# A norm's factor spread over the partitions: diagonal and matmul, or a store to DRAM and a broadcast load

## The chip, the cores and the metric

The kernel runs on one core of a Trainium2 chip. The metric is the device time of one execution in microseconds, the median of several. Five engines work side by side, each through its own list of instructions in order: TensorE (PE in the profile, its weight loads PEld), VectorE (DVE), ScalarE (ACT), GpSimd (POOL) and SyncE (SP), which here only issues DMAs. An instruction that has to wait holds up everything behind it on its engine. ACT issues a few DMAs as well.

## What is computed

A trunk of two layers over 1024 tokens of width 1024. Each layer normalizes x, projects it, runs token attention (windowed in the first layer, a two-dimensional neighbourhood in the second) beside a cross-attention into 256 memory tokens, projects back, normalizes again and applies a SwiGLU of width 2816. A last norm ends it.

```python
def rmsnorm(x, g):
    x32 = x.astype(jnp.float32)
    y = x32 * lax.rsqrt(jnp.mean(x32 * x32, axis=-1, keepdims=True) + EPS)
    return (y * g.astype(jnp.float32)).astype(x.dtype)

mem_n = rmsnorm(mem, norm_mem)
for i in range(DEPTH):
    h = rmsnorm(x, norm_mix[i])
    ...
    x = x + jnp.concatenate([y_tok, y_mem], axis=-1) @ w_out[i]
    h = rmsnorm(x, norm_ffn[i])
    gu = h @ w_gate_up[i]
    x = x + (jax.nn.silu(gu[..., :D_FF]) * gu[..., D_FF:]) @ w_down[i]
return rmsnorm(x, norm_final)
```

The change touches only how the factor of a norm, one number for each token, reaches the places where it is multiplied in.

## The kernel before

**Layout.** x is held transposed: features on the 128 partitions in eight tiles `x[k]`, tokens along the free dimension, in two halves `f` of 512 tokens (`HS`). A float32 product is made of three matmuls of a rounded part and a rest: `hi` (ACT rounds) and `lo` (DVE subtracts, in some places POOL) split every operand, weights too, and L140, L1079 and L1510 are the three matmuls per block of the projections, of the gate-and-up products and of the down products.

**A norm.** `Norm.add` squares a tile on ACT and sums squares on DVE. `Norm.sums` lets PE sum over the partitions (L213, out `st`, 128 tokens on the partitions, one column per block of 128 tokens), DVE adds epsilon (L233, `nv`), POOL takes the power -1/2 (L234, `nr`). The factor now lies with one token on each partition. To bring it to every partition with tokens along the free dimension, DVE writes a diagonal matrix (L237, `diag`), and `Norm.scale` multiplies it with a matrix of ones on PE (L249, `bc`, a PSUM bank). `raw`, `split`, `finish` and `right_sides` multiply x by gain and factor from that bank (L256, L270, L1523, L1269). A norm over 512 tokens is called with n=512, the memory norm has 256, and the last two quarters (`ends`) have 256 each: twelve norms, twelve `bc` products.

**Which norm is where.** At the start the first half's projections are made of x without its factor; `unit_scale`, a copy of `bc` in SBUF, is multiplied into their results later (L488, `first_sums`, and L650). The memory norm's factor is copied to `scale` (L486). The second half's first norm is used in `split` for `hT`. In each layer the norm of the first half of the tokens before the SwiGLU is summed while the second half's output projection runs (L1245), and at the end of each layer the first half's next norm is summed within the last of seven down products (`i == 6`), which goes through six groups `g` of weight tiles (two each, the last one; PE takes group 4 together with group 5).

**Order.** The program is written in the order of the code, and the scheduler of the framework then sets each engine's list by its own estimate of when operands are ready, so neighbours on an engine may come from places of the code that lie apart. Tiles come from pools with a set number of buffers; a load into a buffer waits until the last reader of its previous content is done. Weight tiles are loaded by SP into a `raw` buffer (five of them in this part of a layer, shared with the output tiles `o`), split by ACT and DVE into one of three `whl` buffers, and then used by PE.

Of the kernel before, what the change touches and what calls it, by code (L numbers as in the profile page):

```python
# [9 lines left out]
F32 = mybir.dt.float32  # L10
# [7 lines left out]
P = 128  # L18
# [3 lines left out]
HS = 512  # L22
# [19 lines left out]
def trunk_kernel(ctx: ExitStack, tc: tile.TileContext, a: dict, out: bass.AP):  # L42
# [17 lines left out]
    nc = tc.nc  # L60
# [17 lines left out]
    memk_d = dr.tile([2, 2, P, 2 * NM], F32, name="memk_d")  # L78
    memv_d = dr.tile([2, P, S], F32, name="memv_d")
    bias_d = dr.tile([NH, P, 3 * P], F32, name="bias_d")  # L80

    ident = cst.tile([P, P], F32, name="ident")
    gains = cst.tile([P, 6, NK], F32, name="gains")
# [13 lines left out]
    def temp(name="t2k", n=HS):  # L97
        t = phase[0].tile([P, HS], F32, tag="t2k", name=name, bufs=phase[1])
        return t[:, :n] if n != HS else t
# [85 lines left out]
    class Norm:  # L185


        def __init__(self, n=HS, summed=NK, bank=ps_t):
            self.n, self.acc, self.xs, self.st, self.dg = n, [], {}, None, None
            self.summed, self.bank = summed, bank  # L190

        def add(self, xk, k=None):
# [27 lines left out]
            nc.vector.tensor_tensor(one, one, sq, op=ALU.add)  # L220
            self.acc.append(one)

        def sums(self):

            n, nb = self.n, self.n // P
            if len(self.acc) > 1:
                self.merge()
            for sq in self.acc:
                self.mean(sq)
            st = self.st  # L230
            v = sp.tile([P, 4], F32, tag="nv", name="nv", bufs=2)
            r = sp.tile([P, 4], F32, tag="nr", name="nr", bufs=2)
            nc.vector.tensor_scalar(v[:, :nb], st[:, :nb], EPS, None, op0=ALU.add)  # L233
            nc.gpsimd.tensor_tensor(r[:, :nb], v[:, :nb], neg_half[:, :nb], op=ALU.pow)  # L234
            self.r = r
            self.dg = temp("diag", n)
            nc.vector.tensor_tensor(  # L237
                self.dg.rearrange("p (b q) -> p b q", q=P),
                ident.unsqueeze(1).to_broadcast([P, nb, P]),
                r[:, :nb].unsqueeze(2).to_broadcast([P, nb, P]),  # L240
                op=ALU.mult,
            )

        def scale(self, bank=ps_o):

            if self.dg is None:
                self.sums()
            bc = bank.tile([P, HS], F32, tag="O" if bank is ps_o else "T", name="bc")[:, : self.n]
            nc.tensor.matmul(bc, ones, self.dg, start=True, stop=True)  # L249
            return bc  # L250
# [9 lines left out]

        def split(self, which, hs, lag=0):

            if self.dg is None:
                self.sums()
            for _ in range(lag):
                yield
            bc = self.scale()
            for k in range(NK):
                h = temp("h")
                nc.vector.scalar_tensor_tensor(  # L270
                    h, self.xs[k], gains[:, which, k : k + 1], bc, op0=ALU.mult, op1=ALU.mult
                )
                t = hp.tile([P, 2, HS], F32R, tag="h", name="hT")
                hi(t[:, 0], h)
                lo(t[:, 1], h, t[:, 0])
                hs[k] = t
                yield
# [9 lines left out]
    with tc.tile_pool(name="mp", bufs=1, reuse_waits="tile") as mp:  # L287
# [105 lines left out]
        run(steps(sums[1], wf[1], hT[0]))  # L393
        last = steps(sums[2], wf[2], hT[0])
        run_some(last, 4)
        norms[0].sums()
        mh = []
        mhl = mp.tile([P, NK, 2, NM], F32R, name="mhl")

# [64 lines left out]
        for i in range(8):  # L464
# [9 lines left out]
                split_wm(i + 2)  # L474
            mem_dense(i)
            if i == 0:
                nc.scalar.copy(unit_scale, norms[0].scale())
                norms[1].xs = {k: x[k][1] for k in range(NK)}
                parts = total(norms[1], [xp[k, 1] for k in range(0, NK, 2)])
                run_some(parts, 3)  # L480
            if i == 1:
                run(parts)
                run(total(mem_norm, [memt.rearrange("p k t -> p (k t)")[:, c : c + HS] for c in range(0, 2 * D, HS)], HS))
                mem_norm.sums()
            if i == 2:
                nc.scalar.copy(scale, mem_norm.scale())  # L486
                for n in range(3):
                    nc.vector.tensor_tensor(first_sums[n], sums[n], unit_scale, op=ALU.mult)  # L488
            if i == 3:
                norms[1].sums()  # L490
                nc.vector.tensor_scalar(nsink, sink, -1.0, None, op0=ALU.mult)
                todo = (None for j in range(4) for _ in finish_wm(j))
            if i == 4:
# [26 lines left out]
    for layer in range(2):  # L520
# [467 lines left out]
        with (  # L988
# [241 lines left out]
            for f in range(2):  # L1230
                for m in range(NK):
# [13 lines left out]
                    if f == 0 and m < NK - 1:  # L1245
                        load_y(1, pairs[m])
                    if f == 1 and m == 0:
                        norms[0].sums()
                        parts = norms[0].raw(2 + layer)
                    if f == 1:  # L1250
                        for _ in range(int(m > 0) + int(m == 6)):
                            k = next(parts)
                            B[k // 4][k % 4] = pair(x[k][0], h_op(k))
                        if 1 <= m <= 2:
# [259 lines left out]

            def finish(norm):

                norm.sums()
                yield
                bc = norm.scale()
                for k in range(NK):  # L1520
                    if k % 2 == 0:
# [58 lines left out]
            for at_, (i, g) in enumerate(dorder):  # L1580
# [15 lines left out]
                for c in quarter if last and not is_a else (slice(0, HS),):  # L1596
                    for m in range(4):
# [6 lines left out]
                        if c is quarter[1]:  # L1604
                            if m == 1:
                                end = finish_end(quarter[0])
                            if m > 0:
                                run_some(end, 1)
                if i == 6 and g > 0:
                    if g == 1:  # L1610
                        parts = norms[0].split(1, hT[0], 1) if is_a else finish(norms[0])
                    run_some(parts, 3 if g > 1 else 1)
                    if g < 5:
                        if is_a:
                            norms[1].add(x[g - 1][1], g - 1)
                        for c in () if is_a else quarter:
# [97 lines left out]
```

## Time and profile before

| | |
|---|---|
| median of 3 runs | 2120.81 us (2120.08 to 2121.54) |
| the profiled execution's own time | 2121.35 us |
| its span in the profile | 2119.5 us |
| PE busy | 2094.4 us (99%) |
| DVE busy | 1522.0 us (72%) |
| ACT busy | 1067.0 us (50%) |
| POOL busy | 575.1 us (27%) |
| moved by DMA | 287.28 MB, mean 136 GB/s |

The span runs from the first instruction to the end of the last one. A row of the timeline gives a start, a length, an engine, a line, the operation and its tiles and how many equal instructions were merged; in brackets the idle time of the engine before them and what ended it. SPq and ACTq are the sequencers of SP and ACT, that is, the issue of a DMA. Starts of matmuls are recorded, their ends are modelled. A float32 product such as `bc` is recorded as two matmuls.

### The profile page before, as it was taken

To read this page: it belongs to the slowest core of one execution; us is meant where nothing else is said; L and a number is where in the kernel's file an instruction comes from. 1 tells how busy PE (TensorE), PEld (TensorE's weight loads), DVE (VectorE), ACT (ScalarE), POOL (GpSimd) and SP (SyncE) were. 2 spreads that over 40 slices of the span, in tenths; PEclk is the share of its full clock that TensorE was granted. 3 is DMA by queue.
4 is the path that set the end of the run, shared out by engine and by line. 5 is a ranking of instruction groups with operands and counts; after the bars stand their busy time and mean duration, and the time that the engine had idled before them with its cause. 6 is when DMAs were issued, how large, how long until landed. Compare 5 with 4: busy or idle time off the path is not lost.

```text
span 2119.5 us, 29023 instructions
## 1 busy us (share of the span) xinstructions
PE 2094.4 (99%) x10316; PEld 1750.1 (83%) x10316; DVE 1522.0 (72%) x2477; ACT 1067.0 (50%) x2035; POOL 575.1 (27%) x614
## 2 busy tenths in 40 slices
PE   9999999999999999999999999999999999999997
PEld 7788888878888888888888888888788888888886
DVE  7787887787666666866776666667986666667675
ACT  6687775444434334344466665654543434344442
POOL 0344330234444430000233223203243444400000
PEclk9999999999999999999999999999999999999998
DMA  6421128332333227865232222275232333277562
GB/s 232 145 82 50 31 95 274 99 111 103 109 114 105 91 105 254 312 217 206 79 109 68 69 71 78 64 268 149 75 110 105 109 115 109 86 253 265 200 220 85
DMA packets 120913, 287.28 MB, mean 136 GB/s; under 512 B 12224, under 2 KB 20672, under 8 KB 120768
## 3 DMA queue, kind: packets, MB, share of 16 engines
q1 hardware_dynamic: 112880, 271.63, 38.1%
q10 hardware_dynamic: 7888, 13.79, 1.7%
q8 instruction: 82, 1.34, 0.3%
q14 instruction: 63, 0.52, 0.1%
HBM read 210.40 MB, written 68.94 MB: 132 GB/s over the span
## 4 chain that ended last, share of the span: by engine, by line
PE 91%; DVE 3%; ACT 2%; DMA 1%; issue 1%; POOL 1%; DVEq 0%; ACTq 0%; SPq 0%; POOLq 0%
PE X L1079 17%; PE Y L1079 16%; PE mm L140 15%; PE X L1510 11%; PE Y L1510 8%; PE po L140 8%; PE O L787 3%; PE S L724 3%; PE pT L767 3%; PE X L1161 2%; PE Y L1161 2%; PE mm L426 1%; DMA wd_kept<-in_w_dn 1%; PE bc L249 0%; POOL wS L1036 0%
## 5 line engine op out<-in xcount | busy, mean ns | idle before, releaser
L1079 PE MATMUL Y<-hB,wgu 128*128 128x512 f32 x1056 | 255.6, 391 | 0.8 <-ACT c L1099 0.8
L1079 PE MATMUL X<-hB,wgu 128*128 128x512 f32 x1056 | 254.8, 391 | 0.0
L1510 PE MATMUL X<-hB,wd 128*128 128x512 f32 (+1 forms) x1092 | 243.8, 384 | 0.9 <-DVE x L1474 0.9
L109 DVE TENSOR_TENSOR wgu<-wS,wgu 128x1024 fp32r<-128x1024 f32 (+1 forms) x124 | 153.0, 1234 | 121.7 <-ACT wgu L106 121.3
L1510 PEld LDWEIGHTS X<-hB,wd 128*128 128x128 f32 x1092 | 200.2, 188 | 41.7 <-issue 2.2
L1079 PEld LDWEIGHTS Y<-hB,wgu 128*128 128x128 f32 x1056 | 196.8, 188 | 43.4 <-ACT c L1099 1.6
L1079 PEld LDWEIGHTS X<-hB,wgu 128*128 128x128 f32 x1056 | 196.0, 188 | 39.8
L752 POOL TENSOR_SCALAR p<-p,stat 128x384 f32<-128x384 f32 (+1 forms) x256 | 139.5, 564 | 315.0 <-DVE stat L749 208.7
L140 PE MATMUL mm<-hT,wqk 128*128 128x512 f32 x672 | 199.2, 405 | 0.0
L106 ACT CAST wgu<-wS 128x1024 fp32r<-128x1024 f32 (+1 forms) x124 | 114.2, 923 | 149.7 <-POOL wS L1036 124.5
L140 PE MATMUL po<-yT,wo 128*128 128x512 f32 x768 | 185.7, 394 | 0.0
L1510 PE MATMUL Y<-hB,wd 128*128 128x512 f32 x792 | 180.7, 389 | 0.0
L1510 PEld LDWEIGHTS Y<-hB,wd 128*128 128x128 f32 x792 | 148.6, 188 | 31.5 <-DVE x L1474 0.4
L234 POOL TENSOR_TENSOR nr<-nv,neg_half 128x4 f32<-128x4 f32 (+1 forms) x12 | 13.4, 1116 | 586.5 <-DVE nv L233 582.6
L140 PEld LDWEIGHTS po<-yT,wo 128*128 128x128 f32 x768 | 142.4, 188 | 30.0 <-issue 1.0
L1079 PE MATMUL X<-hT,wgu 128*128 128x512 f32 x624 | 150.2, 391 | 0.0
L106 ACT CAST hB<-b_raw 128x512 fp32r<-128x512 f32 x154 | 89.3, 618 | 112.7 <-DMA b_raw<-b_d 95.9
L1036 POOL TENSOR_TENSOR wS<-wgu_raw 128x512 f32<-128x512 f32 x44 | 61.0, 1387 | 295.1 <-DVE wgu L109 295.1
L1079 PEld LDWEIGHTS X<-hT,wgu 128*128 128x128 f32 x624 | 116.9, 188 | 26.1
L739 ACT ACTIVATE p<-p,stat 128x256 f32<-128x256 f32 (+1 forms) x192 | 112.5, 587 | 49.2 <-DVE stat L735 47.0
L109 DVE TENSOR_TENSOR pl<-pT,ph 128x384 fp32r<-128x384 f32 (+1 forms) x256 | 118.8, 493 | 18.5 <-ACT ph L106 15.4
L1079 PE MATMUL Y<-hT,wgu 128*128 128x512 f32 x528 | 129.9, 391 | 0.0
(208 smaller groups left out, 4204.3 us busy)
## 6 DMA issues: line engine op xcount, KB each, us to landing
wgu_raw<-in_w_gu SPq DMA_DIRECT2D x92, 512.0 KB
wd_raw<-in_w_dn SPq DMA_DIRECT2D x70, 512.0 KB
b_raw<-b_d SPq DMA_DIRECT2D x70, 512.0 KB
b_d<-c SPq DMA_DIRECT2D x88, 256.0 KB
b_d<-t SPq DMA_DIRECT2D x66, 256.0 KB
wo_raw<-in_w_out SPq DMA_DIRECT2D x32, 512.0 KB
xr_d<-x ACTq DMA_DIRECT2D x32, 256.0 KB
xr<-xr_d SPq DMA_DIRECT2D x16, 512.0 KB
```

Of the source, the lines that this page charges most:

```text
L106: nc.scalar.copy(dst, src)
L109: (eng or nc.vector).tensor_tensor(dst, src, h.bitcast(F32), op=ALU.subtract)
L140: nc.tensor.matmul(ps[:, :n], l, r, start=start and i == 0 and j == 0, stop=stop and i == len(order) - 1 and j == 2,)
L724: nc.tensor.matmul(s_[:, :n], Q[self.h][:, qb * P : (qb + 1) * P], k, start=j == 0, stop=j == 1)
L739: nc.scalar.activation(p[:, :n], p[:, :n], AF.Exp, bias=m1, scale=-1.0, accum_out=s1)
L752: nc.gpsimd.tensor_scalar(p[:, :n], p[:, :n], ri[:, i : i + 1], 1.0, op0=ALU.mult, op1=ALU.mult)
L767: nc.tensor.transpose(tr[:, j * P : (j + 1) * P], p[:, j * P : (j + 1) * P], ident)
L787: nc.tensor.matmul(o[:, c0 : c0 + w * P], self.value(j), t[:, s0 : s0 + w].rearrange("p j q -> p (j q)"), start=j == js[0] and t is self.p ...
L1036: sub = lambda o, p_, q_: nc.gpsimd.tensor_tensor(o, p_, q_, op=ALU.subtract)
L1079: nc.tensor.matmul(ps, l, r, start=n in (0, 1, 3, 6) and k == 0 and i == 0, stop=k == 3 and i == 2, skip_group_check=True,)
L1161: nc.tensor.matmul(bank[:, at : at + h2], l, r, start=start and k == 0 and i == 0, stop=stop and k == 1 and i == 2, skip_group_check=True,)
L1510: nc.tensor.matmul(bank[:, c], l, r, start=i in (0, 1, 3, 6) and p == 0 and n == 0, stop=p == HF - 1 and n == 2, skip_group_check=True,)
```

## The change

`Norm.sums` takes a tile `into`. With it, no diagonal is written: SP stores the factors `r` (128 partitions by four, or by two) to a row `r_d` in DRAM, one token after the other, and loads that row into `into`, the same row for each of the 128 partitions. `scale` then returns this SBUF tile and issues no matmul. Seven of the twelve norms are called so: the first half's at the start (into `unit_scale`), the memory norm (into `scale`), the second half's at the start, the first half's before the SwiGLU of each layer, and the first half's at the end of each layer. The copies of `bc` to `unit_scale` and `scale` on ACT go. The five others keep the diagonal and the matmul.

Three places of the code move. At the start the second half's `sums` comes at `i == 2` in place of 3. Before the SwiGLU, the scaled tiles are made from `m == 2` on in place of 1, with two at m = 4 and 6. At the end of a layer `sums` comes after group 0 of `i == 6` in place of group 1, and the first use one step later than before.

```diff
+    r_d = [dr.tile([1, HS], F32, name=f"r_d{i}") for i in range(7)]
+    used = []
...
-        def sums(self):
+        def sums(self, into=None):
...
             self.r = r
+            if into is not None:
+                row = r_d[len(used)]
+                used.append(row)
+                nc.sync.dma_start(row[:, :n].rearrange("o (b p) -> p (o b)", p=P), r[:, :nb])
+                nc.sync.dma_start(into[:, :n], row[:, :n].to_broadcast([P, n]))
+                self.bc = into[:, :n]
+                return
             self.dg = temp("diag", n)
...
         def scale(self, bank=ps_o):
+            if self.bc is not None:
+                return self.bc
...
-        norms[0].sums()
+        norms[0].sums(unit_scale)
...
             if i == 0:
-                nc.scalar.copy(unit_scale, norms[0].scale())
...
-                mem_norm.sums()
+                mem_norm.sums(scale)
             if i == 2:
-                nc.scalar.copy(scale, mem_norm.scale())
+                norms[1].sums(temp("bc"))
...
             if i == 3:
-                norms[1].sums()
...
                     if f == 1 and m == 0:
-                        norms[0].sums()
+                        norms[0].sums(temp("bc"))
...
-                        for _ in range(int(m > 0) + int(m == 6)):
+                        for _ in range(int(m > 1) + int(m in (4, 6))):
...
             def finish(norm):
-                norm.sums()
-                yield
+                norm.sums(temp("bc"))
+                for _ in range(2):
+                    yield
...
-                if i == 6 and g > 0:
-                    if g == 1:
-                        parts = norms[0].split(1, hT[0], 1) if is_a else finish(norms[0])
+                if i == 6:
+                    if g == 0:
+                        if is_a:
+                            norms[0].sums(temp("bc"))
+                            parts = norms[0].split(1, hT[0], 2)
+                        else:
+                            parts = finish(norms[0])
                     run_some(parts, 3 if g > 1 else 1)
-                    if g < 5:
+                    if 0 < g < 5:
```

What the scheduler makes of it is seen in the engines' lists. First PE at the start, where it runs the memory projections (`mm<-mhl,wm`) and then the second half's first projections (`mm<-hT,wf`). Before:

```order
L426 MATMUL mm<-mhl,wm 128x256 x24
L249 MATMUL bc<-diag,ones 128x512
L426 MATMUL mm<-mhl,wm 128x256 x42
L213 MATMUL st<-inv_d,sq 128x1 x2
L426 MATMUL mm<-mhl,wm 128x256 x18
L249 MATMUL bc<-diag,ones 128x256
L426 MATMUL mm<-mhl,wm 128x256 x12
L213 MATMUL st<-inv_d,sq 128x1 x4
L426 MATMUL mm<-mhl,wm 128x256 x26
L249 MATMUL bc<-diag,ones 128x512
L426 MATMUL mm<-mhl,wm 128x256 x53
```

and the same stretch now:

```order
L437 MATMUL mm<-mhl,wm 128x256 x68
L215 MATMUL st<-inv_d,sq 128x1 x2
L437 MATMUL mm<-mhl,wm 128x256 x6
L215 MATMUL st<-inv_d,sq 128x1 x4
L437 MATMUL mm<-mhl,wm 128x256 x107
```

Three `bc` products are gone, and the sums of the second half's norm (the four `st`) follow the memory norm's after 6 matmuls in place of 30.

Second, DVE at the end of the first layer, from the norm's `nv` on; `wd` is the split of down weights, `h` and `hT` are the normalized tiles for the next layer and their splits, `hB` the split of a right side. Before:

```order
L233 TENSOR_SCALAR nv<-st 128x4
L237 TENSOR_TENSOR diag<-ident,nr 128x512
L109 TENSOR_TENSOR wd<-wd_raw,wd 128x1024
L109 TENSOR_TENSOR wd<-wd_raw,wd 128x512
L270 SCALAR_TENSOR_TENSOR h<-x_00_8726,gains,bc 128x512
L270 SCALAR_TENSOR_TENSOR h<-x_10_8731,gains,bc 128x512
L270 SCALAR_TENSOR_TENSOR h<-x_20_8736,gains,bc 128x512
L109 TENSOR_TENSOR hT<-h,hT 128x512 x3
```

and now:

```order
L235 TENSOR_SCALAR nv<-st 128x4
L111 TENSOR_TENSOR wd<-wd_raw,wd 128x1024
L281 SCALAR_TENSOR_TENSOR h<-x_00_8725,gains,bc 128x512
L111 TENSOR_TENSOR wd<-wd_raw,wd 128x1024
L111 TENSOR_TENSOR hT<-h,hT 128x512
L281 SCALAR_TENSOR_TENSOR h<-x_10_8730,gains,bc 128x512
L281 SCALAR_TENSOR_TENSOR h<-x_20_8735,gains,bc 128x512
L281 SCALAR_TENSOR_TENSOR h<-x_30_8740,gains,bc 128x512
L111 TENSOR_TENSOR hT<-h,hT 128x512 x2
L111 TENSOR_TENSOR wd<-wd_raw,wd 128x512
L281 SCALAR_TENSOR_TENSOR h<-x_40_8504,gains,bc 128x512
L281 SCALAR_TENSOR_TENSOR h<-x_50_8509,gains,bc 128x512
```

The splits of the last two weight tiles (128x1024, then 128x512) now stand behind `h`, the first reader of the loaded factor; on PE the norm's `st` comes 20 matmuls earlier here (after 28 of the last product in place of 48), and the next layer's second norm has its `st` after 15 matmuls of `mm<-hT,wf` in place of 29.

Third, SP at the end of the program: `wd_raw` are down weights, `b_raw` right sides, `out` the result. Before:

```order
L1376 DMA wd_raw<-in_w_dn 128x2x512
L1432 DMA b_raw<-b_d_99 128x512
L1376 DMA wd_raw<-in_w_dn 128x512
L1528 DMA out<-o 128x2x512 x4
L1555 DMA out<-o 128x2x256 x5
```

and now:

```order
L1385 DMA wd_raw<-in_w_dn 128x2x512
L1441 DMA b_raw<-b_d_99 128x512
L241 DMA r_d_109<-nr 128x4x1
L242 DMA bc<-r_d_109 128x512
L1538 DMA out<-o 128x2x512
L1385 DMA wd_raw<-in_w_dn 128x512
L1538 DMA out<-o 128x2x512 x3
```

The last load of weights stood ahead of all output; it now stands behind the factor's store, its load and the first output store, which needs the first two scaled tiles.

4 lines of the change are left out of this document (2 added, 2 removed).

## The prediction

> **What bounds the kernel now.** I read the page's busy times first, then its chain of work, then PE's own waits.
>
> ```profile
> PE 2094.4 (99%) x10316; PEld 1750.1 (83%) x10316; DVE 1522.0 (72%) x2477; ACT 1067.0 (50%) x2035; POOL 575.1 (27%) x614
> ...
> PE 91%; DVE 3%; ACT 2%; DMA 1%; issue 1%; POOL 1%; DVEq 0%; ACTq 0%; SPq 0%; POOLq 0%
> ```
>
> PE is busy for 2094.4 of 2119.5 us, and 91% of the chain that ended last runs on it. DVE, the next, is at 72%.
>
> ```profile
> PE pT L767 <- DVE pl L109: 3.2, 8, 0.8
> ...
> PE bc L249 <- DVE diag L237: 2.1, 3, 1.7
> ```
>
> The first is the longest kind of PE's waits; the second are waits of `bc` itself for the diagonal. So time goes where PE has less to issue or waits less, and other engines matter through deadlines that PE sets. The norm's own products:
>
> ```profile
> L249 PE MATMUL bc<-diag,ones x24: 380/591/767, 29.7 to 2110.8; 128*128 128x512 f32 x18, 128*128 128x256 f32 x6
> ```
>
> Twelve products are 24 records; fourteen of them go. Their lengths are modelled, so I price them by the starts around them.
>
> **What goes from PE: four products in steady streams.** The first norm before a SwiGLU and its surroundings, and last a piece of the chain of work:
>
> ```profile
> 356.62 5.73 PE L140 MATMUL po<-yT,wo 128*128 128x512 f32 x24
> 357.04 1.02 POOL L234 TENSOR_TENSOR nr<-nv,neg_half 128x4 f32<-128x4 f32 x1 [45.25 <-DVE nv L233]
> ...
> 362.19 1.02 PE L249 MATMUL bc<-diag,ones 128*128 128x512 f32 x2
> 362.38 0.69 DVE L1242 TENSOR_TENSOR x<-po,x 128x512 f32<-128x512 f32 x1
> 362.64 3.55 PE L140 MATMUL po<-yT,wo 128*128 128x512 f32 x13
> ...
> 363.21 32.69 PE po L140 x144
> ```
>
> 24 matmuls from 356.62 to 362.19 are 0.232 us each. `bc` holds the next start back to 362.64, 0.45 us. Of the 13 that follow, the last starts some 0.39 us before the end of the row, so 12 steps take 3.16 us where 2.78 are normal: another 0.38. One product costs 0.83 us, with no wait in it. The same norm of the second layer and the two at the ends of the layers stand in the same kind of stream: 4 x 0.83 = 3.3 us.
>
> **Three products at the start.**
>
> ```profile
> 29.74 1.02 PE L249 MATMUL bc<-diag,ones 128*128 128x512 f32 x2
> 30.19 5.59 PE L426 MATMUL mm<-mhl,wm 128*128 128x256 f32 x42
> 36.34 0.58 PE L213 MATMUL st<-inv_d,sq 128*128 128x1 f32 x4 [0.56 <-DVE sq L374]
> 36.78 2.38 PE L426 MATMUL mm<-mhl,wm 128*128 128x256 f32 x18
> 39.43 0.67 PE L249 MATMUL bc<-diag,ones 128*128 128x256 f32 x2 [0.26 <-DVE diag L237]
> 39.75 1.78 PE L426 MATMUL mm<-mhl,wm 128*128 128x256 f32 x12
> ...
> 45.61 1.10 PE L249 MATMUL bc<-diag,ones 128*128 128x512 f32 x2
> 46.14 6.92 PE L426 MATMUL mm<-mhl,wm 128*128 128x256 f32 x53
> ```
>
> The normal step here is 0.12 us: of the 18 from 36.78 on the last starts some 0.28 us before the row's end, and 17 steps take 2.10. By the same reckoning the first costs 0.45 + (5.31 - 41 x 0.12) = 0.84; the memory norm's 0.32 + 0.18 and its wait for the diagonal, 0.26, makes 0.76; the third 0.53 + 0.40 = 0.93. Together 2.5 us. But this stretch ends in a chain of DVE and ACT work:
>
> ```profile
> 47.56 2.06 DVE L270 SCALAR_TENSOR_TENSOR h<-x,gains,bc 128x512 f32<-128x512 f32 x3
> ...
> 55.15 3.36 PE L140 MATMUL mm<-hT,wf 128*128 128x512 f32 x14
> ...
> 59.25 0.69 DVE L109 TENSOR_TENSOR hT<-h,hT 128x512 fp32r<-128x512 f32 x1
> ```
>
> From the first `h` to the last `hT` DVE takes 59.94 - 47.56 = 12.4 us, and PE asks for that last tile after 21 matmuls, at 55.15 + 21 x 0.233 = 60.04: a margin of 0.1 us. PE now comes 2.5 us earlier. The third `bc` (0.9) lies behind the release on which the last weight split ahead of `h` waits, so DVE comes only about 1.7 us earlier, and 0.8 us is handed back. What stays is 1.7 us.
>
> **One wait goes with it.** At the start of the second layer the second norm's `st` waits for DVE, and its `bc` (this one stays) for the diagonal:
>
> ```profile
> 1035.83 0.97 PEld L213 LDWEIGHTS st<-inv_d,sq 128*128 128x128 f32 x8 [0.33 <-DVE sq L220]
> ...
> 1039.48 1.12 PE L249 MATMUL bc<-diag,ones 128*128 128x512 f32 x2 [0.18 <-DVE diag L237]
> ```
>
> The diagonal has 24 matmuls of cover now instead of 10, and DVE starts on `h` earlier, so I take 0.33 + 0.18 = 0.5 us as gained. It is bounded by 0 and by some 0.8.
>
> **What is added: a round trip through DRAM.** Neither the store of 512 separate floats nor the broadcast load occurs in the trace. The nearest rows are a store that a load waits for, a load that an engine waits for, and a queue's mean:
>
> ```profile
> 65.72 0.33 ACTq L442 DMA_DIRECT2D memk_d<-mkh  x1
> 70.02 1.35 SPq L632 DMA_DIRECT2D mKH<-memk_d  x2
> SPq L632 <- DMA memk_d<-mkh: 3.5, 1, 3.5
> ...
> 356.00 0.33 SPq L1226 DMA_DIRECT2D wgu_raw<-in_w_gu  x1
> 360.03 1.05 ACT L106 CAST wgu<-wgu_raw 128x1024 fp32r<-128x1024 f32 x1 [2.40 <-DMA wgu_raw<-in_w_gu]
> ...
> 930.81 3.52 DMA wd_raw<-in_w_dn
> q10 hardware_dynamic: 7888, 13.79, 1.7%
> ```
>
> A store of 256 KB took 4.3 us until SP could issue the load behind it; loads of 512 KB took 4.0 us in a busy stretch and 3.5 in a quieter one. So R, from `nr` to the landed factor, is at most about 8.3 us if the small store costs no more than that store. The other end: without the data time (at the page's mean of 136 GB/s a 256 KB store moves 1.9 us, a 512 KB load 3.9) hardly 3 us would be left. q10's packets take 1.7% x 16 x 2119.5 / 7888 = 0.073 us each; 32 pieces per DMA engine are then at most 2.3 us, likely less, as these packets hold 1.7 KB on average. I take **R = 6.5 us**, nearer the upper rows, because all of them are landings really waited for; 3 and 8.3 stay as ends.
>
> The trace has no row of 4-byte pieces. [...]
>
> What stands behind the waits: SP's load of the factor waits for the store, and DVE's first reader for the load. Before the SwiGLU `nr` is ready at 358.1, so the factor lands near 364.6; DVE idles from the end of its `x` of the second tile (363.1) until then. Behind it are weight splits for tiles one and two steps of 5.6 us away and the next `x`, which PE finishes only at 362.64 + 24 x 0.232 = 368.2: hidden, with 3 us to spare. The scaled tiles, made from m = 2 on, are all asked for after the last `po` at 395.9, and the last of them keeps its step. On SP the `x` and `wo_raw` loads slip by about 2 us; PE has no wait on either in its table. At the start a load of weights waits on SP for `nr`:
>
> ```profile
> 21.43 13.65 SPq L302 DMA_DIRECT2D wm<-in_w_mem  x4
> ...
> 33.66 1.05 ACT L106 CAST wm<-wm 128x1024 fp32r<-128x1024 f32 x1
> ```
>
> The first of those four goes out near 26.5 instead of 21.4, and ACT splits that tile at 33.7. ACT loses two copies, DVE seven diagonals, all beside PE's work; that the factor is read from SBUF instead of PSUM I count as nothing for the same reason.
>
> Three places have real deadlines.
>
> ```profile
> 997.59 10.89 PE X L1510 x48
> 1004.20 1.22 DVE L109 TENSOR_TENSOR wd<-wd_raw,wd 128x1024 fp32r<-128x1024 f32 x1 [0.73 <-ACT wd L106]
> ...
> 2071.83 10.89 PE X L1510 x48
> 2077.06 0.34 SPq L1376 DMA_DIRECT2D wd_raw<-in_w_dn  x1
> 2078.43 1.23 DVE L109 TENSOR_TENSOR wd<-wd_raw,wd 128x1024 fp32r<-128x1024 f32 x1 [0.84 <-ACT wd L106]
> 2089.99 4.70 DVE L1523 SCALAR_TENSOR_TENSOR o<-x,gains,bc 128x512 f32<-128x512 f32 x7 [1.94 <-PE bc L249]
> ```
>
> *Start:* PE reaches the second half's `st` near 36.7 (the memory norm's at 36.34 less the first 0.84, then 0.5 and six matmuls) and is through 0.9 later; 0.16 for `nv` and 1.0 for the power put `nr` near 38.9. DVE is free for `h` near 45.8: room for R = 6.9. *End of layer one:* `st` follows 28 matmuls of 0.227 us, DVE is free at 1005.4, `nr` comes at 1006.7. From the first `h` to `hB` DVE has six `h` (0.67 each), three `hT`, `wd` in both sizes and `hB`, 8.1 us; PE needs that near 997.59 + 96 x 0.227 + 0.8 + 6 x 0.23 = 1021.6: room for 6.8. *End of the program:* `nr` at 2080.9, the last `wd` needed by the same count near 2095.1. Ahead of its split DVE has eight `o` (0.67), a `wd` (1.15), a `sq` (0.4), with the split itself 7.7 us: room for 6.4. Another path is as long: two `o`, the output store's issue, `wd_raw` issued and landing in 3.5 us, ACT, DVE, about 7.4. Before, `wd_raw` was issued at 2077.06 and had 12 us to spare; this cover is gone. With R = 6.5 the three cost 0 + 0 + 0.1 us.
>
> **The sum.** 3.3 + 2.5 - 0.8 + 0.5 - 0.1 = 5.4 us (5.45 unrounded), against the profiled execution's 2121.35 us, its 1.85 us around the span kept: 2115.9. That execution is 0.54 us above the median of the runs, so the median should be **2115.4 us**. About 0.2%, 4.2 us, is what a measurement of this kernel can tell from no change.
>
> **The rivals.**
>
> *The gain is handed back to the round trip.* R near 8.3, the upper rows: late by 1.4, 1.5 and 1.9 us at the three places, 4.8 in all, 4.7 more than counted; 2115.4 + 4.7 = 2120.1. For it: every DMA row above is 3.5 us or more, and SP's two issues and the semaphore hops come on top. Against it: that store moves 128 times the 2 KB of this one, and DMA is quiet at the end of the program.
>
> *The start gives nothing.* If the chain from `h` to `hT` and the puts after it keep their times, all of 2.5 us is lost rather than 0.8: 2115.4 + 1.7 = 2117.1. For it: the margin of 0.1 us. Against it: the DVE chain itself begins behind work that waits for PE.
>
> *Everything comes through.* Start whole, deadlines met, 0.8 at the norm of layer two: 2115.4 - 1.2 = 2114.2; with `bc` priced a little higher, 2113.8.
>
> *Slower: 512 pieces are dear.* The mechanism is the same three deadlines, with the last weight tile behind the factor as its hardest place. From R = 6.9 on each further us costs up to three; the sum of lateness is 3R - 20.1. The gain is used up at R = 8.5, and the run is 0.2% slower from R = 10.0 on. A piece at 0.25 us instead of 0.073 makes the store 8 us and R near 12: 15.9 us late, 2115.4 + 15.8 = 2131.2. For it: no row shows such a store. Against it: 0.073 us is a mean over much larger packets.
>
> *It doesn't do what it says.* Of PE's list seven products are gone, so this could only be a PE that isn't the bound; 99% busy speaks against it, and I give it no chance of its own.
>
> **How the numbers follow.** Forecast 0.50, everything through 0.12, start gives nothing 0.12, handed back 0.17, slower 0.09. Forecast and "everything" are faster by over 0.2% except for an edge of the forecast (gains under 4.2 us), which I put at 0.05; a little of "handed back" and "start" lies beyond the bound on that side, 0.02: faster 0.59, same 0.31, slower 0.10, of which 0.01 is from "handed back". Range: 2113.6, just below "everything", to 2120.1, "handed back"; this leaves out the slower case and little else.
>
> **What would show it.** Right: fourteen fewer `bc` records, the stretch from the output projection to the first gate product shorter by 0.83 us in both layers, PE without a new wait at `mm<-hT,wf` above about 1 us, and no wait of PE at the last group of the last down product. The load of `bc` behind its store tells R. Wrong would be: PE waiting for `wd` or `hB` at either end of a layer, DVE idle before L256 beyond 368, or R over 8 us.

## The result and the profile after

The changed kernel takes **2159.06 us** (median of 5 runs, 2157.69 to 2160.35) against 2120.81 of the kernel before (2120.08 to 2121.97): the ratio is 1.0177, 95% interval 1.0166 to 1.0188. It is 38 us slower where the forecast had 5.4 us of gain.

The page of the changed kernel, its busy times and its chain of work:

```profile
PE 2102.5 (97%) x10302; PEld 1755.1 (81%) x10302; DVE 1524.5 (71%) x2470; ACT 1065.1 (49%) x2033; POOL 579.2 (27%) x614
...
PE 83%; DVE 6%; DMA 5%; ACT 2%; issue 2%; POOL 1%; SPq 0%; DVEq 0%; ACTq 0%; POOLq 0%
```

PE has fourteen records fewer than before (10302 against 10316), as the seven products that go are fourteen records. All the same its busy time rose by 8 us and its share of the span fell to 97%. On the chain PE gave up eight points, most of them to DVE and DMA. What PE waited for (total us, times, longest):

```profile
PE mvT L460 <- ACT mt L456: 7.3, 1, 7.3
PE po L142 <- DVE wo L111: 4.9, 5, 1.7
PE X L1519 <- DVE wd L111: 4.7, 3, 2.1
PE st L215 <- DVE sq L222: 3.1, 2, 2.1
...
PE X L1519 <- ACT wd L108: 2.7, 1, 2.7
PE X L1519 <- ACT hB L108: 2.4, 1, 2.4
```

None of these kinds led the table before. They stand at all the places of the change: `mvT` at the start, `po` ahead of the SwiGLU, `X` and `st` at the ends of the layers. Behind them stand SP and DVE (L241 is the store, L242 the load):

```profile
SPq L242 <- DMA r_d<-nr: 47.5, 6, 10.0
...
DVE x L267 <- DMA bc<-r_d: 19.4, 2, 9.7
DVE h L281 <- DMA bc<-r_d: 18.7, 2, 14.8
...
DVE o L1533 <- DMA bc<-r_d: 13.1, 1, 13.1
```

SP waited some 8 us for the end of each store, and DVE 9.7 to 14.8 us for the factor at each of the four places behind the start. The end of layer one in the order of time, first POOL, SP and DVE, then PE:

```profile
1018.76 1.94 POOL L236 TENSOR_TENSOR nr<-nv,neg_half 128x4 f32<-128x4 f32 x1 [210.13 <-DVE nv L235]
1020.73 0.38 SPq L241 DMA_DIRECT2D r_d<-nr  x1
1029.87 0.33 SPq L242 DMA_DIRECT2D bc<-r_d  x1
1034.65 0.75 DVE L281 SCALAR_TENSOR_TENSOR h<-x,gains,bc 128x512 f32<-128x512 f32 x1 [14.82 <-DMA bc<-r_d]
...
1036.59 1.20 PE L1519 MATMUL X<-hB,wd 128*128 128x512 f32 x4 [2.09 <-DVE wd L111]
1040.20 0.79 PE L1519 MATMUL X<-hB,wd 128*128 128x512 f32 x1 [2.42 <-ACT hB L108]
1042.92 9.52 PE L1519 MATMUL X<-hB,wd 128*128 128x512 f32 x29 [1.92 <-DVE hB L111]
```

From `nr` at 1020.70 the store takes 9.1 us until SP can issue the load, the load 4.8 us until DVE goes on: a round trip of 13.9 us where 6.5 was forecast and 6.8 was free. In the tail, where nothing else stands in the queues, it is hardly shorter:

```profile
2110.84 0.37 SPq L241 DMA_DIRECT2D r_d<-nr  x1
2118.99 0.33 SPq L242 DMA_DIRECT2D bc<-r_d  x1
2123.96 1.42 DVE L1533 SCALAR_TENSOR_TENSOR o<-x,gains,bc 128x512 f32<-128x512 f32 x2 [13.08 <-DMA bc<-r_d]
```

That is 8.15 + 4.97 = 13.1 us. The third loss shows in the table of stretches. A row has the stretch, its length, the busy time of PE, PEld, DVE, ACT and POOL, then the granted clock of PE, the DMA engines' busy share and the GB/s moved. The clock is the column to look at, which in the kernel before was 1.00 in every stretch that was read ahead of its last 30 us:

```profile
1036.00:1050.00 14.00, 9.08 (x24) 6.55 (x25) 14.00 (x20) 7.85 (x14) 4.83 (x4) 0.63 0.11 35
1050.00:1064.00 14.00, 11.91 (x50) 9.58 (x49) 8.26 (x12) 4.36 (x6) 7.91 (x9) 0.88 0.39 131
2125.00:2140.00 15.00, 10.05 (x56) 9.56 (x57) 10.03 (x20) 2.29 (x5) 0.00 (x0) 0.66 0.44 157
```

Behind PE's stops the clock is 0.63, 0.88 and 0.66 on average. Read in steps of 2 us, it is 0.50 from 1040 to 1048 us, also when PE works again: from 1044 to 1048 PE is busy without a break and has 6 matmuls in each 2 us, from 1050 to 1054, at 1.00, it has 10.

### The profile page after: what moved, and what is told of

Read it like the earlier page. It is cut to its first block, busy times and chain, and to the rows that moved or that the text cites. A ratio compares the mean times of both kernels' runs of the same rounds, so it can differ in the third digit from the quotient of the medians.

```text
span 2156.6 us, 28999 instructions
## 1 busy us (share of the span) xinstructions
PE 2102.5 (97%) x10302; PEld 1755.1 (81%) x10302; DVE 1524.5 (71%) x2470; ACT 1065.1 (49%) x2033; POOL 579.2 (27%) x614
## 2 busy tenths in 40 slices
DMA packets 125360, 288.99 MB, mean 134 GB/s; under 512 B 15776, under 2 KB 24352, under 8 KB 125216
## 4 chain that ended last, share of the span: by engine, by line
PE 83%; DVE 6%; DMA 5%; ACT 2%; issue 2%; POOL 1%; SPq 0%; DVEq 0%; ACTq 0%; POOLq 0%
PE X L1088 16%; PE Y L1088 16%; PE mm L142 14%; PE X L1519 9%; PE Y L1519 8%; PE po L142 5%; PE O L796 3%; PE S L733 3%; PE pT L776 3%; PE X L1170 2%; DMA r_d<-nr 2%; PE Y L1170 2%; DMA bc<-r_d 1%; DVE sq L222 1%; DVE wgu L111 1%
## 5 line engine op out<-in xcount | busy, mean ns | idle before, releaser
L1519 PE MATMUL X<-hB,wd 128*128 128x512 f32 (+1 forms) x1092 | 250.0, 390 | 12.8 <-DVE wd L111 4.7
L1519 PEld LDWEIGHTS X<-hB,wd 128*128 128x128 f32 x1092 | 204.9, 194 | 55.4 <-DVE wd L111 5.6
```

What stands on the lines that cost most here:

```text
L1519: nc.tensor.matmul(bank[:, c], l, r, start=i in (0, 1, 3, 6) and p == 0 and n == 0, stop=p == HF - 1 and n == 2, skip_group_check=True,)
```

## The experiments

**One place at a time.** Each of four kernels takes store and load at one place and keeps diagonal and product elsewhere; the edit for the end of layer one (the norm is begun after group 0, as in the change):

```
                 if is_a:
+                    norms[0].sums(temp("bc"))
-                    parts = norms[0].split(1, hT[0], 1)
+                    parts = norms[0].split(1, hT[0], 2)
```

> Only the three norms at the start (norms[0] of the first tokens, the memory norm, norms[1]) take the store and the load; all other places keep diagonal and product. Theory A (each place pays by itself: the round trip takes 13 to 15 us where some 7 were free, the in-order VectorE and SP stand behind it, TensorE then waits and loses half its clock for some 10 us after the stop): TensorE waits about 7 us at the product mvT, the granted clock is near 0.8 just behind it, and the whole is about 2128 us, +7 us on the kernel before. Theory B (the loss is not made here; the start was ahead by 2 us and is only late because the store stands in SP's queue behind other transfers, and the lateness is made good later, as the attention has spare time): 2119 to 2122 us.

> Only the norm of the first half of the tokens ahead of the SwiGLU, in both layers, takes the store and the load. Theory A: VectorE stands some 10 us before its first scaled tile and SP some 8 us before the load, the splits of wo come late, and TensorE loses 5 to 6 us in each layer: about 2132 us, +11. Theory B (the forecast's own term: the round trip is hidden there, and what the whole change lost there was only the queueing behind the other places' transfers): 2119 to 2121 us.

> Only the norm at the end of layer one takes the store and the load. Theory A: VectorE stands 14 to 15 us, TensorE waits four times for some 8.5 us in all (for wd, hB and sq), and its granted clock is halved for one or two pieces of 10 us behind it: about 2134 us, +13. Theory B (TensorE's slower clock in the whole change comes from a limit over the whole run, not from the stops; a single place doesn't set it off): the waits alone, about 2128 us, with the granted clock at 1.0 behind the boundary.

> Only the final norm takes the store and the load; nothing behind it can absorb anything. Theory A: round trip 13 us against some 6.4 free, waits of 2.0, 2.7 and 0.7 us and a half clock behind them: about 2128 us, +7. Theory B (the round trip is long only since the queues hold other transfers of the change): the trip takes 6 to 9 us by itself and the time is 2120 to 2123 us. If the four single places add up to +38 us, places are independent; if they add up to much less, each makes the others worse.

Measured: 2129.77, 2132.45, 2134.96 and 2129.63 us against 2121.14, ratios 1.0038 (1.0023 to 1.0053), 1.0053 (1.0038 to 1.0068), 1.0062 (1.0047 to 1.0077) and 1.0037 (1.0023 to 1.0051). That is 8.6 + 11.3 + 13.8 + 8.5 = 42.2 us for 38 together: theory A. Each place loses by itself, the SwiGLU, costed at nothing, too.

**Is it the pieces?** The factor is turned and stored as 4 pieces of 512 bytes:

```
-nc.sync.dma_start(row[:, :n].rearrange("o (b p) -> p (o b)", p=P), r[:, :nb])
+nc.tensor.transpose(tr[:nb, :P], r[:, :nb], ident)
+nc.scalar.copy(rt[:nb], tr[:nb, :P])
+nc.sync.dma_start(row[:, :n].rearrange("o (b p) -> (o b) p", p=P), rt[:nb])
```

> The whole change, but the factor is first turned on TensorE (128 partitions by 4 to 4 partitions by 128), copied by ScalarE, and stored as 4 pieces of 512 bytes in place of 512 pieces of 4 bytes; the load is the same. In the changed kernel the store in the tail, with nothing else in the queue, moved its last 4-byte piece about 1.2 us after its first, and the load was still let go only 8.2 us after the store. Theory A (the time of the store is the end of a transfer to DRAM, whatever its pieces): 8 to 9 us from store to load remain, the turning adds about 1 us, and the time is 2155 to 2168 us. Theory B (the 512 small pieces are what is dear): 3 to 4.5 us from store to load, the round trip near 9 us, and the time is 2132 to 2145 us.

Measured: 2130.93 us, 1.0048 (1.0033 to 1.0063): theory B, a little below its range. The page of the whole change counts 15776 packets under 512 bytes, 3552 more than the kernel before (12224); here it is 12362, 138 more. SP in the tail, the store and then the load:

```profile
2091.43 0.27 SPq L245 DMA_DIRECT2D r_d<-rt  x1
2092.61 0.33 SPq L249 DMA_DIRECT2D bc<-r_d  x1
```

The store's end is there after 1.2 us instead of 8.15. What is left of the loss has other waits, among them 5.5 us in which PE waited in five places for `nr` to turn it.

**Is it the order?** The same places and lags, without DRAM:

```
-nc.sync.dma_start(row..., r...)
-nc.sync.dma_start(into[:, :n], row[:, :n].to_broadcast([P, n]))
+nc.tensor.matmul(prod, ones, dg, start=True, stop=True)
+nc.scalar.copy(into[:, :n], prod)
```

> The whole change in its order (the steps begun at the same places, the same lags), but without DRAM: the factor is spread by diagonal, product and a copy by ScalarE straight away, at the point where the store stood. Theory A (the round trip is the cost, the moved steps cost nothing): 2118 to 2124 us. Theory B (the order is the cost: steps begun a group earlier put instructions of VectorE and SP ahead of what TensorE needs): 2135 us or more.

Measured: 2123.56 us, 1.0012 (1.0003 to 1.0022): theory A. The small rest can be PE's, which waits 2.3 us for the diagonals right behind `st`; that wasn't tried apart.

**Another issuer.** Store and load issued by GpSimd (`nc.gpsimd.dma_start` for both):

> The whole change, but the store and the load are issued by GpSimd, behind its own power, and not by SP: SP never stands behind them, so that the loads of x and wo and the others go out as before. Theory A (what costs is VectorE, which stands in order before the first instruction that reads the factor): the round trip and VectorE's waits stay at 13 to 15 us, only the wm, wo and x loads come earlier, and the time is 2148 to 2160 us. Theory B (what costs is SP's queue that stands behind the load): below 2135 us.

Measured: 2172.40 us, 1.0241 (1.0226 to 1.0257). Slower than either theory had it: it frees SP, but GpSimd then waits 33.9 us for the ends of its own stores, and DVE's waits for the factor grow: 28.2 us for `h`, 23.5 for `x` and 13.7 for `o`, against 18.7, 19.4 and 13.1 in the whole change.

**PE kept busy.** Eighteen products that nobody reads, ahead of the place where PE stood in e3_end1:

```
+for _ in range(18):
+    nc.tensor.matmul(spare[:, :NM], ones, gains_wide, start=True, stop=True)
```

> The norm at the end of layer one alone (as in e3_end1, 2134.96 us), and 18 products of 128x256 that nobody reads are added on TensorE just ahead of the wd products where it stood still (3.8, 1.5 and 1.9 us). They change nothing in the result. Theory A (the granted clock falls because TensorE stood still): with TensorE kept busy the clock stays at 1.0 from 1018 to 1042 us; in e3_end1 it was 0.66 from 1030 to 1036. The 18 products take the place of idle time, and the whole is the same as or up to 4 us shorter than e3_end1, 2130 to 2136 us, in spite of the added work. Theory B (the clock falls for another reason at this place, as when the weights change or the DMA is busy): 0.66 stays there, and the added work makes it 2138 to 2145 us.

The two stretches, first of e3_end1, then of this kernel:

```profile
1024.00:1030.00 6.00, 2.87 (x5) 1.45 (x5) 6.00 (x11) 3.75 (x7) 0.00 (x0) 0.50 0.16 45
1030.00:1036.00 6.00, 5.30 (x16) 4.26 (x17) 6.00 (x9) 3.89 (x7) 3.76 (x4) 0.66 0.00 0
```

```profile
1024.00:1030.00 6.00, 6.00 (x30) 5.22 (x29) 6.00 (x11) 3.76 (x7) 0.00 (x0) 1.00 0.19 57
1030.00:1036.00 6.00, 6.00 (x28) 4.93 (x27) 6.00 (x9) 3.89 (x7) 3.77 (x4) 1.00 0.00 0
```

The clock is 1.00 instead of 0.50 and 0.66: here it falls because PE stands still. The time missed theory A's range: 2138.96 us, 1.0081 (1.0064 to 1.0098). DVE was as late as before, so PE's stop moved on to the next layer's `st`, 6.7 us instead of 3.2, and the added 7.9 us of products were not paid back. Keeping PE busy held the clock at 1.00 in these two stretches and didn't take the wait away.

**128 pieces.** Again the whole change, with 16 bytes for each partition:

```
-row[:, :n].rearrange("o (b p) -> p (o b)", p=P)
+row[:, :n].rearrange("o (p b) -> p (o b)", p=P)
```

> The whole change, with the same 2 KB stored as 128 pieces of 16 bytes (a partition's four factors side by side) in place of 512 of 4 bytes; the load is unchanged, so that the factors reach other tokens than their own. In e5_contig the wait from store to load fell to 1.2 us in the tail and at the end of layer one with 4 pieces of 512 bytes; with 512 pieces it is 8.2 to 9.2 us. Theory A (the time goes by the number of pieces): 1.2 + 7.5 x 124/508 = 3.0 us from store to load in the tail, and 2130 to 2140 us. Theory B (every piece below some size makes the end of the store late, whatever their number): 7 to 9 us from store to load, and 2150 to 2160 us.

Measured: 2126.10 us, 1.0028 (1.0016 to 1.0039), below both ranges. Store, load and first reader in the tail:

```profile
2088.11 0.34 SPq L241 DMA_DIRECT2D r_d<-nr  x1
2091.01 0.32 SPq L245 DMA_DIRECT2D bc<-r_d  x1
...
2094.29 1.41 DVE L1536 SCALAR_TENSOR_TENSOR o<-x,gains,bc 128x512 f32<-128x512 f32 x2 [6.15 <-DMA bc<-r_d]
```

From store to load 2.9 us here, 3.0 expected. But at the end of layer one the same kernel's load is let go after 1.4 us, and so is the one in the tail of e14_copy, a kernel further below with the same 128 pieces:

```profile
1008.67 0.33 SPq L241 DMA_DIRECT2D r_d<-nr  x1
1010.09 0.33 SPq L245 DMA_DIRECT2D bc<-r_d  x1
```

```profile
2080.14 0.34 SPq L241 DMA_DIRECT2D r_d<-nr  x1
2081.57 0.32 SPq L245 DMA_DIRECT2D bc<-r_d  x1
```

So it is 1.2 us with 4 pieces, 1.4 to 2.9 with 128, and 8.15 with 512 (8.7 in the tail of e4_tail). Theory B falls: pieces of 16 bytes don't bring the long end. Theory A is right in that fewer pieces are far cheaper, but its straight line isn't shown, as 128 pieces mostly cost hardly more than 4. With 2 KB each time, the number of the pieces and their size change together; 128 pieces of 4 bytes weren't tried. The one store of another number doesn't speak for the number alone: in e1_start the memory norm's 256 pieces of 4 bytes took 10.4 us, the two stores of 512 around it 11.6 and 8.3, all among other loads.

**Stores that nobody waits for.** The kernel before, with the store added to `sums` and nothing else:

```
 self.r = r
+nc.sync.dma_start(row[:, :n].rearrange("o (b p) -> p (o b)", p=P), r[:, :nb])
```

> The kernel before, with diagonal and product at all places, and ten stores of a factor in 512 (the memory norm 256) pieces of 4 bytes that nobody loads or waits for. Theory A (a store only costs him who waits for its end): 2119 to 2124 us. Theory B (the small pieces hold up SP or the DMA queue, so that the loads of x, wo and wm behind them come some 7 us late): 2128 us or more, and the loads behind a store are issued or land late in the trace.

Measured: 2135.47 us, 1.0068 (1.0052 to 1.0083). My theory A fell here: ten stores without a reader cost 14.8 us. Whether the pieces do it, or SP's waiting for each factor, is asked again in e15_store16 below.

**The trip covered.** The norm ahead of the SwiGLU alone; SP issues the load with `x` of step 2, and DVE makes the scaled tiles in steps 4 to 7. The first added line holds the load back by writing one column of `bc0`, the second does so with the tiles:

```
+if f == 1 and m == 2:
+    nc.vector.tensor_scalar(bc0[:, :1], x[m][f][:, :1], 1.0, None, op0=ALU.mult)
+    norms[0].load()
+if f == 1 and m == 3:
+    nc.vector.scalar_tensor_tensor(bc0[:, :1], x[m][f][:, :1], 0.0, bc0[:, :1], op0=ALU.mult, op1=ALU.add)
-for _ in range(int(m > 0) + int(m == 6)):
+for _ in range(int(m > 3) + int(m in (4, 5, 6, 7))):
```

> Only the norm ahead of the SwiGLU, in both layers, and the round trip is covered: SP issues the load only with x of step 2 (so that it doesn't stand behind the store), and the scaled tiles are made from step 4 on, two in each step, instead of from step 1. Theory A (the trip of 13 to 15 us costs nothing where it has 17 us of cover, and two products of 0.83 us go): no wait of VectorE over 2 us for the factor, no wait of TensorE for wo, 2117 to 2121 us, against 2132.45 of e2_ffn. Theory B (the moved scaled tiles crowd VectorE in steps 4 to 7 and the SwiGLU starts late, or the small pieces cost wherever they stand): 2124 us or more.

Measured: 2133.64 us, 1.0066 (1.0054 to 1.0079), no better than e2_ffn. DVE no longer waits for the factor, but SP's rows and the stretch behind its store say where the time goes (the last three columns are the granted clock, the DMA engines' busy share and the GB/s moved):

```profile
358.79 0.38 SPq L241 DMA_DIRECT2D r_d<-nr  x1
359.23 0.53 SPq L1033 DMA_DIRECT2D x<-in_x  x1
359.81 0.42 SPq L1240 DMA_DIRECT2D wgu_raw<-in_w_gu  x1
362.91 0.33 SPq L116 DMA_DIRECT2D wo_raw<-in_w_out  x1
```

```profile
362.00:370.00 8.00, 8.00 (x37) 6.64 (x36) 3.65 (x5) 1.58 (x2) 0.00 (x0) 1.00 0.68 38
```

The kernel before in the same stretch:

```profile
362.00:370.00 8.00, 8.00 (x35) 6.27 (x34) 7.79 (x10) 4.50 (x6) 2.92 (x2) 1.00 0.55 177
```

SP doesn't stand behind the store: 0.4 us later it issues the next load, and five are issued by 365.8. Yet from 362 to 370 us they move 38 GB/s, where 177 were moved before. The store holds up what comes behind it.

**Another queue.** As e11_late, with the store on ScalarE's queue (`nc.scalar.dma_start`), at 357.65:

> The same as e11_late (2133.64 us), but the store in 512 pieces is issued by ScalarE, on whose queue only the copies of x go out, and no longer by SP. In e11_late SP issued the loads of x, wgu and wo behind the store at once, and they moved 14 to 50 GB/s from 362 to 370 us where the kernel before moved 221 to 239. Theory A (the small pieces hold the queue on which they stand): the loads of SP move at 200 GB/s or more in those windows, TensorE doesn't wait for wo, and the time is 2118 to 2123 us. Theory B (they hold the DMA engines that all queues share, or the memory): the same hole in those windows, and 2129 to 2136 us.

```profile
362.00:370.00 8.00, 8.00 (x37) 6.63 (x36) 2.71 (x4) 1.57 (x2) 0.66 (x1) 1.00 0.71 32
```

The same hole, 32 GB/s, with no small piece on SP's queue; 2135.02 us, 1.0065 (1.0051 to 1.0079). Theory B: it isn't the queue on which the pieces stand. Whether they hold the DMA engines or the memory, which theory B left open, isn't shown.

**A form to use, and why it failed at first.** The two SwiGLU norms and the final norm alone, 128 pieces, read from SBUF with a stride:

```
-self.bc = into[:, :n]
+self.bc = into[:, :n].rearrange("p (q b) -> p b q", b=nb)
```

> A version meant to be used: only the norms ahead of the SwiGLU and the final norm take the store and the load; the factor is stored in 128 pieces of 16 bytes and loaded in that order (factor b of partition p at 4p + b), and VectorE reads it from SBUF with a stride of 16 bytes, so that each token gets its own. In e9_p16 TensorE had no new wait at these three places. Theory A (the trip of 7 to 8 us is hidden there, three products of 0.83 us go, the stride costs VectorE nothing): 2117 to 2121 us. Theory B (the queue is still held some 2 us for 128 pieces and VectorE stands 3.5 us: as much is lost as is won, or the strided reading is slower than 743 ns per tile): 2121 to 2126 us.

Measured: 2127.13 us, 1.0028 (1.0018 to 1.0037), 1 us above theory B's range. Two of its causes are seen: DVE stands 3.8 us at each SwiGLU norm, and a strided product takes 1130 ns. The first row is the scaled tiles of this kernel, the second those of the next one (min, median and max ns), which turns the factor once:

```
+nc.vector.tensor_scalar(self.flat.rearrange("p (b q) -> p b q", q=P),
+                        self.bc[:, : self.n].rearrange("p (q b) -> p b q", q=P), 1.0, None, op0=ALU.mult)
```

```profile
L273 DVE SCALAR_TENSOR_TENSOR x<-x,gains,bc x16: 1110/1130/1158, 366.7 to 1464.7; 128x512 f32<-128x512 f32 x16
```

```profile
L275 DVE SCALAR_TENSOR_TENSOR x<-x,gains,flat x16: 736/743/1780, 371.7 to 1459.3; 128x512 f32<-128x512 f32 x16
```

> The same as e13_best (2127.13 us), but VectorE turns the loaded factor into the order of the tokens once at each place, with one 128x512 instruction of some 0.7 to 1.2 us, and its 24 products read it without a stride. In e13_best they took 1130 ns each against 743 ns in the kernel before, 24 x 0.39 = 9.3 us of VectorE. Theory A (the strided reading was what e13_best lost by): no product over 760 ns but beside GpSimd, TensorE without new waits, and 2117 to 2121 us. Theory B (the 128 pieces or VectorE's stop of 3.8 us cost it): 2123 to 2128 us again.

Measured: **2119.78 us**, 0.9998 (0.9989 to 1.0007) of the kernel before, within theory A's range. That the stride was the whole loss isn't shown, as the scheduler's lists changed too. Ahead of the SwiGLU the first reader of the factor now stands behind a split of `wo` and the next `x`, and DVE no longer waits for the factor there (7.7 us in the two layers of e13_best). In the tail SP issues the last load of weights right behind the factor's load, at 2081.99; in e13_best it stood behind the first output store, at 2095.28. The longest products of the second row take 1780 ns. In the changed kernel one takes as long (1.78 us from 389.56 on, where the median is 746 ns), while POOL writes its `wS` from 387.20 to 390.78.

The best form can't be told from no change. Its profiled span, 2116.5 us, is 3.0 shorter than before, but that execution is the fastest of its eleven. PE's rows of the output projection, first before, then here:

```profile
356.62 5.73 PE L140 MATMUL po<-yT,wo 128*128 128x512 f32 x24
362.19 1.02 PE L249 MATMUL bc<-diag,ones 128*128 128x512 f32 x2
362.64 33.25 PE L140 MATMUL po<-yT,wo 128*128 128x512 f32 x144
395.73 2.95 PE L1079 MATMUL X<-hB,wgu 128*128 128x512 f32 x12
```

```profile
356.42 38.38 PE L142 MATMUL po<-yT,wo 128*128 128x512 f32 x168
394.63 2.95 PE L1098 MATMUL X<-hB,wgu 128*128 128x512 f32 x12
```

From the first of these 168 matmuls to the first `X` it is 39.11 us before and 38.21 here; in the second layer 39.12 and 38.21. A product in a steady stream is worth 0.90 us; the forecast had 0.83.

**Pieces or SP's waits?** e10_store with pieces of 16 bytes:

> As e10_store (2135.47 us): the kernel before with ten stores that nobody loads, now in 128 pieces of 16 bytes in place of 512 of 4 bytes. Theory A (the hold goes by the number of pieces): a quarter of e10_store's 14.8 us or less, 2120 to 2125 us, and no hole behind the store at 358 us. Theory B (the hold doesn't go by pieces; e10_store lost by SP's waiting for the factor, 86 us in ten waits, which is the same here): 2130 us or more.

Measured: 2120.59 us, 0.9998 (0.9989 to 1.0007). Theory A as to the time: SP waits for the factor as long as there (84.8 us against 86.4), and it costs nothing that can be measured. So e10_store lost by its pieces; here too their number and their size changed together. The stretch behind the store, first e10_store (store at 364.32), then this kernel (store at 357.56):

```profile
366.00:372.00 6.00, 6.00 (x26) 4.62 (x25) 3.99 (x7) 3.98 (x6) 0.00 (x0) 1.00 0.99 49
```

```profile
358.00:364.00 6.00, 6.00 (x26) 4.61 (x25) 4.59 (x6) 3.13 (x4) 0.00 (x0) 1.00 0.82 229
```

49 GB/s against 229, and in the first the DMA engines' records are 99% busy all the same. The two stretches don't lie equally far behind their stores; from 359.24 to 365.24, as far behind as the first, this kernel moves 199 GB/s. A short hole is left, 78 GB/s from 360 to 362.

## Why the prediction was wrong

**The step that failed is R = 6.5 us, and in it the price of the store.** I bounded 512 pieces of 4 bytes by rows of large transfers, and took a piece for 0.073 us on one of 16 engines in parallel, at most 2.3 us together. From the store's issue to the load's it was 8.15 to 9.2 us at the four places behind the start and 7.3 to 11.4 at the start, among other loads. With the load's 5 to 6 us that is a trip of 13 to 15, outside the bounds of 3 to 8.3. The time doesn't lie in moving the pieces: in the tail their last record ends some 2.1 us after the issue, inside what I had counted, and the load is let go 6 us later. None of the rows from which I took R has such an end.

**What the pieces hold up was missing altogether.** The forecast asked only who waits for the factor. Stores that nobody waits for cost 14.8 us in ten places (e10_store), and nothing measurable with a quarter of the pieces, each four times as large (e15_store16). This is why "hidden, with 3 us to spare" ahead of the SwiGLU, which I costed at nothing, cost 11.3 us, and why covering the trip didn't help (e11_late). The slip of the `x` and `wo_raw` loads that I put at 2 us is a hole of 8.

**The slower rival named the right cause and was too small.** It put 512 dear pieces at R near 12 and 2131.2 us. Its 0.25 us a piece isn't what the tail shows: from 2110 to 2114 us 528 packets under 512 bytes take 6.8% of 16 engines' 4 us, 0.008 us each, and the load is let go only 8.15 us after the store. Its own formula, 3R - 20.1, with the 13.9 of layer one's end in all three deadlines gives 21.6 us late, 2115.4 + 21.5 = 2136.9; the run has 22 more. The rooms of the three deadlines were about right: with trips of 13.2, 13.9 and 13.1 us they make PE 6.3, 7.1 and 6.7 us late, and it waited 7.3 us for `mvT`, 6.4 in three steps at the end of layer one and 5.4 at the end of the program. Two things aren't in the formula: the held transfers, and the clock. PE's stops of 1.5 to 3.8 us, several close together, are followed by stretches at half clock, and the four quoted stretches of e3_end1 and e8_fill show that it is the stops that bring it.

An estimate from the busy times and spans before and after: PE's idle time rose by 29.0 us (54.1 against 25.1), its busy time by 8.1 although products worth some 6 us went. That is about 14 us of slower work beside 29 us of waiting. It isn't a clean division, as the ends of matmuls are modelled and a held load also makes the stop that halves the clock.

PE's first stop in e3_end1, of 3.79 us, and the clock of 0.50 from 1024 to 1030 us stand together: the row of PE is

```profile
1024.38 2.08 PE L1524 MATMUL X<-hB,wd 128*128 128x512 f32 x4 [3.79 <-DVE wd L111]
```

How long a stop has to be isn't shown: in the whole change the clock is 1.00 from 1036 to 1038 us, behind a stop of 2.09 us, then 0.59 from 1038 to 1040 and 0.50 from 1040 on, within and behind a second stop of 2.42. Another issuer for the store didn't help the loads either: from 362 to 370 us 32 GB/s are moved in e12_actq, where the store stands on ScalarE's queue, and 38 in e11_late, where it stands on SP's.

**What was right, and the smaller terms.** Fourteen records go, a product in a steady stream is worth 0.9 us, and the moved steps by themselves cost little (e6_moved, +2.5 us with seven products and copies back in). With the pieces made fewer and DVE's reading kept straight, three norms came out level with the kernel before (e14_copy). The start and the end of layer one stay too tight for any form that was run: with 128 pieces, where the tail's trip is 2.9 + 3.3 = 6.2 us, PE still waited 3.9 us for `mvT` and 4.7 for `st`.

The 0.5 us that the wait of `st` at layer two was to give became one of 2.1 us, as the last squares came late with everything else on DVE. What the three products at the start give wasn't tried by itself.

Of "what would show it", all three signs of the wrong case came: PE waiting for `wd` and `hB` at the ends of the layers, DVE idle ahead of the scaled tiles (old L256) until 381.03, and R over 8 us.

## What to carry to other kernels

Count the pieces of a transfer before its bytes: 2 KB in 512 pieces of 4 bytes held up SP's loads for some 8 us, whether it stood on SP's queue (38 GB/s from 362 to 370 us in e11_late) or on ScalarE's (32 in e12_actq), and also where nobody waited (49 from 366 to 372 in e10_store); the same 2 KB in 128 pieces of 16 bytes cost nothing measurable (e15_store16, 0.9998). Ask of an added transfer not only who waits for it, but what else is on its way then. And where one engine is 99% busy, price its stops twice: once for the wait, and once for the clock behind it, here 0.50 for 8 us (1040 to 1048) behind stops of 2.09 and 2.42 us.

## What the runs showed that was not expected

In the tail of the changed kernel the queues are empty, and the pieces' own records are short. The DMA engines' busy share in tenths, in 40 slices of 0.45 us from 2108 to 2126:

```profile
DMA  0000000140000000000000000000002896100000
```

Nearly all of the store's pieces (and a fetch of instructions) lie in two slices, from 2111.15 to 2112.05; a finer view, of 2110 to 2114, counts 528 packets under 512 bytes and has the last ones before 2113. From there to 2119 there is no record of a transfer at all:

```profile
DMA packets 0, 0.00 MB, mean 0 GB/s; under 512 B 0, under 2 KB 0, under 8 KB 0
```

The load was let go only at 2118.99. What fills these 6 us isn't in the records. In e4_tail, with the same store alone, the load is let go 8.7 us after the store's issue. With 4 pieces (e5_contig) the last record lies between 2092.00 and 2092.25 us, and the load follows at 2092.61. A strided operand in SBUF (16 bytes from element to element) made the `scalar_tensor_tensor` of 128x512 on DVE 1130 ns long (e13_best) instead of 743 (e14_copy).
